# Turning group A's attention probabilities on VectorE, with value products in 32-row tiles

## The chip, the cores and the metric

The kernel runs on one core of one Trainium2 chip. Times are device microseconds (us) of one execution. A core has TensorE (PE: matmuls; its weight loads are shown apart as PEld), VectorE (DVE), ScalarE (ACT), GpSimd (POOL) and SyncE (SP, which here only issues DMAs), an on-chip memory SBUF of 128 partitions, and the accumulator memory PSUM with eight banks of 512 float32 columns. TensorE multiplies a stationary operand, loaded ahead as weights, with a moving operand, and sums over the partitions of the two.

## The reference

Two layers of an encoder on 1024 tokens of width 1024. Each layer normalizes, projects into four groups of attention heads (A to D), joins their outputs, projects back and adds, and then applies a squared-ReLU MLP of width 4096. Group A, which the change concerns, has four heads with keys of 96 and values of 64 columns and looks at all 1024 keys:

```python
def one_block(qi):                       # 128 queries at a time
    s = jnp.einsum('bqhd,bkhd->bhqk', qi, k, preferred_element_type=jnp.float32) * scale
    p = jax.nn.softmax(s, axis=-1)
    return jnp.einsum('bhqk,bkhd->bqhd', p.astype(v.dtype), v)
...
mix = jnp.concatenate([rms_norm(y_a, out_g_mla[l]), y_b,
                       rms_norm(y_c, out_g_swa[l]), rms_norm(y_d, out_g_na[l])], axis=-1)
x = x + mix @ w_out[l]
h = rms_norm(x, norm2_g[l])
x = x + jnp.square(jax.nn.relu(h @ w_up[l])) @ w_down[l]
```

All is float32. Group B has two softmaxes per head over all keys, C a band of keys, D a neighbourhood on a grid.

## The kernel before

Everything is planned before anything is emitted. The code calls engine operations on a `Plan`, which only records each as a step with its operands and what it depends on. `Plan.price` gives each step a cost, `Plan.order` then walks forward in time and picks for each engine, out of the steps whose inputs are ready, the one of lowest rank, if the places for its outputs are free; the steps are emitted in that order. A rank comes from the table `SPAN`: the steps of a stage (`"a"` for group A, `"o1"` and `"o2"` for the output projection, and so on) are spread over the stage's two numbers, so that a stage with earlier numbers goes first where both could run. The numbers are priorities and no times. `together()` makes several steps one unit that is emitted without a break.

Places are the SBUF and PSUM spaces that the plan gives out: 40 `pair` places of 1024 float32 columns a partition, 19 `half` of 512, small ones, and the 8 PSUM banks. `Place.tile` chooses the kind by size; a place goes back when the last step that uses its tile is done.

Group A, per head: four loads fill `stack` tiles (high and low parts of queries and keys, 96 rows), one load fills `v` ([128 keys, 8 blocks, 64]). For each of eight tiles of 128 queries, `softmax` runs six score matmuls of 512 columns into two `sb` banks, two VectorE reduces that move a bank to the SBUF tile `p` and keep the minimum (in the profile CUSTOM_DVE_ANT_0, each followed by a short read-out of the accumulator), and one ACT exponential over 1024 columns, which also gives the sum. `dense` then takes two query tiles at a time: eight 128x128 transposes of each on TensorE (`bank<-ident,p`) into `tr` banks, copies of 512 columns to `pt` tiles, in turn by VectorE and ACT (`transposed`), and eight value products with 64 stationary columns and 256 moving ones (`bank<-pt,v`), half of which write PSUM partitions 0 to 63 and half 64 to 127. `pv_out` adds the two halves: ACT copies one to `pvt`, VectorE adds it to the other into `y`. A float32 matmul is two records in the profile (each a weight load and a matmul); float32r, which scores and projections use, is one.

Of the output projection, products with `mix` (the split, normalized group outputs) belonging to groups B, D and C are in `o1`, since they don't need group A; the rest is in `o2`. In the MLP, operands split into a high and a low part lie in `pair` places (`near`, `far`).

Of the kernel before, what the change touches and what calls it, by code (L numbers as in the profile page):

```python
# [266 lines left out]
class Plan:  # L267
# [40 lines left out]
    def add(self, q, op, args, kw):  # L308
# [8 lines left out]
        s.start, s.tiled = None, False  # L317
# [51 lines left out]
    def price(self, s):  # L369
# [24 lines left out]
        if q == "tensor":  # L394
# [27 lines left out]
    def order(self):  # L422
# [30 lines left out]
        self.mode = False  # L453
# [119 lines left out]
    def issue(self, s, t):  # L573
# [13 lines left out]
        if q == "tensor":  # L587
# [13 lines left out]
            s.done = t + occ * (2 if s.tiled else 1) + 180 * (1.5 if slow else 1)  # L601
# [11 lines left out]
class Place:  # L613
# [9 lines left out]
    def tile(self, shape, dt, tag, bufs=None, name=None):  # L623
# [4 lines left out]
        kind = "pair" if n > 512 else "half" if n > P else "row" if n > 16 else "col"  # L628
# [8 lines left out]
class Trunk:  # L637
# [16 lines left out]
    PLACES = {"pair": 40, "half": 19, "row": 3, "col": 30, "bank": 8}  # L654

    def home(self, c):
        if c.kind in self.still:
            return self.still[c.kind][c.slot]
        n = 1024 if c.kind == "pair" else 512
# [239 lines left out]
    def attention(self, l):  # L899
# [51 lines left out]
        with at("open"):  # L951
# [84 lines left out]
        with at("o2"):  # L1036
# [13 lines left out]
    BANKS = {"mm": 8, "tr": 4, "sb": 2, "pv": 2}  # L1050
    EARLY, NP = 4, 6
    WAVES = [(T_BQ[t], T_BK[t], T_BV[t]) for t in range(2)]
# [134 lines left out]
    def latent_up(self, l, lat, rows, qa, ka, va):  # L1187
        nc, d = self.nc, self.d
        rq, rkv = self.big_tile(F, "rq"), self.big_tile(F, "rkv")
# [3 lines left out]
        for i, r in ((0, P), (1, 64), (2, P)):  # L1193
            p = []
            for j in range(2):
                t = self.big_tile(R, "latp")
# [163 lines left out]

    def attn_b(self, l, t, qb, kb, vb, out):
# [53 lines left out]
    def attn_a(self, l, qa, kn, krd, va, ys):  # L1415
# [3 lines left out]
        def head(h):  # L1419
# [13 lines left out]
            v = self.vtile(va[h])  # L1433
# [12 lines left out]
        yield from self.dense([lambda h=h: head(h) for h in range(4)])  # L1446
# [192 lines left out]

    def rows_split(self, t, src, scale=None):  # L1640

        self.split(t[0], t[1], src, scale)
        return t
# [22 lines left out]
    def mlp_up(self, l, acts):  # L1666
# [7 lines left out]
        with self.banks(u=2, p=2, q=2, mm=2):  # L1674
            near = lambda tag: [self.twin("op" + tag, R) for _ in range(4)]
# [118 lines left out]
            places = [near(c) for c in "abc"]  # L1794
# [58 lines left out]
    def mlp_down(self, l, acts):  # L1853
# [4 lines left out]
        with self.banks(u=4, p=4):  # L1858
# [4 lines left out]
            for j in range(4):  # L1863
# [12 lines left out]
                def op(o):  # L1876
                    return [self.rows_split(self.far(), t) for t in raw_op(o)]
# [130 lines left out]
```

## Time and profile before

| | us |
|---|---|
| median of three runs | 2522.7 (2518.65 to 2522.78) |
| profiled execution | 2517.78 |
| its span in the profile | 2516.0 |
| TensorE busy in the span | 2467.4 |
| VectorE / ACT / GpSimd busy | 1909.8 / 1290.5 / 379.7 |
| mean granted TensorE clock | 0.996 |

All helpers record through one line, so every group in the profile has the line L677, and groups are told apart by tile names: `out<-in`. A group's row gives the operation, its shapes, the count, then busy time and the mean ns of one, then the idle time of the engine before it with what ended it. A timeline row gives start, duration, engine and a count of like instructions in a row; its duration goes from the first start to the last end. Durations of matmuls include time in which the next one already streams.

### The profile page before, as it was taken

What the parts mean: (1) busy time and instruction counts of PE and PEld (TensorE: products, weight loads), DVE (VectorE), ACT (ScalarE), POOL (GpSimd) and SP (SyncE); (2) the same over time, 40 slices, a digit from 0 to 9 for tenths busy, and PEclk for the clock granted to TensorE, in tenths of its full rate; (3) what the DMA queues carried; (4) which work ended last, traced back from release to release, by engine and by line L of the source; (5) the groups of instructions that cost most, each with busy time, mean ns of one, the idle gap of its engine ahead of it and who ended that gap; (6) DMA issues with size and microseconds to landing.
All of it is one profiled execution on the core that took longest, in us unless ns stands there. A gap on an engine that the chain in (4) does not pass through costs nothing.

```text
span 2516.0 us, 35396 instructions
## 1 busy us (share of the span) xinstructions
PE 2467.4 (98%) x12332; PEld 1967.1 (78%) x12332; DVE 1909.8 (76%) x3576; ACT 1290.5 (51%) x2397; POOL 379.7 (15%) x258
## 2 busy tenths in 40 slices
PE   8999999999999999999999999999999999999998
PEld 6777776778888887888877777677788888888887
DVE  7767867775877779888777677677678777898887
ACT  4545757653644445444425456666455444444454
POOL 3323224213000000000042231332140000000000
PEclk9999999999999999999999999999999999999999
DMA  5534478622244457444154344885123444665431
GB/s 180 180 112 133 122 218 234 197 80 72 78 165 159 151 202 271 147 142 139 72 182 130 119 117 135 232 255 170 46 70 117 155 155 158 231 231 158 130 105 67
DMA packets 190514, 378.56 MB, mean 150 GB/s; under 512 B 24112, under 2 KB 36352, under 8 KB 190336
## 3 DMA queue, kind: packets, MB, share of 16 engines
q1 hardware_dynamic: 175360, 350.09, 44.6%
q10 hardware_dynamic: 14976, 26.22, 2.7%
q8 instruction: 97, 1.59, 0.3%
q14 instruction: 81, 0.66, 0.1%
HBM read 260.15 MB, written 116.07 MB: 150 GB/s over the span
## 4 chain that ended last, share of the span: by engine, by line
PE 83%; DVE 8%; DMA 4%; ACT 2%; issue 2%; SPq 1%; POOL 0%; DVEq 0%; POOLq 0%; ACTq 0%
PE bank L677 83%; DVE p L677 2%; DVE part L677 1%; SPq L677 1%; ACT p L677 1%; DVE x L677 1%; DMA a<-in_w_down 1%; DVE sq L677 1%; DMA acts<-ev 1%; DVE col L677 0%; DMA latp<-lat 0%; DMA c<-in_w_down 0%; DVE xl L677 0%; DVE ev L677 0%; DVE both L677 0%
## 5 line engine op out<-in xcount | busy, mean ns | idle before, releaser
L677 PE MATMUL bank<-far,wh 128*128 128x512 f32 (+1 forms) x2848 | 870.3, 387 | 1.1 <-ACT wh L677 0.6
L677 PEld LDWEIGHTS bank<-far,wh 128*128 128x128 f32 x2848 | 532.4, 188 | 110.5 <-ACT wh L677 1.4
L677 PE MATMUL bank<-far,wl 128*128 128x512 f32 (+1 forms) x1424 | 550.3, 387 | 2.7 <-DVE wl L677 2.7
L677 ACT ACTIVATE p<-p,col 128x1024 f32<-128x1024 f32 (+2 forms) x320 | 294.6, 921 | 196.3 <-DVE col L677 194.2
L677 POOL TENSOR_TENSOR wl<-ws,wh 128x512 fp32r<-128x512 f32 (+1 forms) x138 | 191.1, 1390 | 1180.2 <-ACT wh L677 1089.8
L677 PEld LDWEIGHTS bank<-far,wl 128*128 128x128 f32 x1424 | 267.4, 188 | 57.9 <-DVE wl L677 3.4
L677 PE MATMUL bank<-stack 96*128 96x512 f32 (+2 forms) x896 | 285.0, 395 | 5.0 <-DVE col L677 2.3
L677 DVE TENSOR_TENSOR x<-bank,x 128x512 f32<-128x512 f32 (+1 forms) x276 | 187.2, 680 | 121.9 <-PE bank L677 121.0
L677 PE MATMUL bank<-ident,p 128*128 128x128 f32 x1376 | 253.6, 276 | 10.4 <-DVE part L677 4.8
L677 PE MATMUL bank<-xh,wh 128*128 128x512 f32 x608 | 250.9, 413 | 3.1 <-ACT wh L677 2.6
L677 PE MATMUL bank<-xh,wl 128*128 128x512 f32 x608 | 250.6, 413 | 1.1 <-POOL wl L677 1.1
L677 PE MATMUL bank<-xl,wh 128*128 128x512 f32 x608 | 250.6, 412 | 0.0
L677 PEld LDWEIGHTS bank<-ident,p 128*128 128x128 f32 x1376 | 171.3, 141 | 59.5 <-issue 10.7
L677 PEld LDWEIGHTS bank<-stack 96*128 96x128 f32 (+1 forms) x896 | 159.3, 189 | 43.8 <-DVE col L677 12.1
L677 ACT ACTIVATE pt<-bank 128x512 f32<-128x512 f32 (+2 forms) x256 | 137.5, 556 | 82.9 <-PE bank L677 75.2
L677 DVE TENSOR_TENSOR wl<-raw,wh 128x512 fp32r<-128x512 f32 x224 | 150.3, 690 | 34.5 <-ACT wh L677 34.0
L677 PE MATMUL bank<-pt,v 128*64 128x256 f32 (+2 forms) x1344 | 173.1, 396 | 2.2 <-ACT pt L677 2.0
L677 ACT ACTIVATE ev<-ev 128x512 f32<-128x512 f32 x128 | 80.6, 632 | 160.3 <-DVE ev L677 155.8
L677 DVE CUSTOM_DVE_ANT_0 p<-bank,zero,col 128x512 f32<-128x512 f32 x192 | 143.8, 749 | 22.2 <-PE bank L677 5.1
L677 PE MATMUL bank<-mix,wh 128*128 128x512 f32 x512 | 160.3, 393 | 0.0
L677 DVE CUSTOM_DVE_ANT_0 p<-bank,zero 128x512 f32<-128x512 f32 x192 | 131.7, 686 | 35.4 <-PE bank L677 34.1
L677 ACT ACTIVATE wh<-raw 128x512 fp32r<-128x512 f32 x224 | 135.4, 621 | 23.8 <-ACT ev L677 10.5
(158 smaller groups left out, 3904.5 us busy)
## 6 DMA issues: line engine op xcount, KB each, us to landing
act<-acts SPq DMA_DIRECT2D x224, 256.0 KB
raw<-in_w_up SPq DMA_DIRECT2D x128, 256.0 KB
acts<-ev SPq DMA_DIRECT2D x128, 256.0 KB
acts<-ev ACTq DMA_DIRECT2D x96, 256.0 KB
ws<-in_w_in SPq DMA_DIRECT2D x76, 256.0 KB
c<-in_w_down SPq DMA_DIRECT2D x64, 256.0 KB
rz<-drows SPq DMA_DIRECT2D x40, 256.0 KB
ws<-in_w_out SPq DMA_DIRECT2D x40, 256.0 KB
```

What stands on the lines that cost most here:

```text
L677: getattr(s.eng.engine, s.op)(*[real(a) for a in s.args], **{k: real(a) for k, a in s.kw.items()})
```

## The change

For group A, `dense` is replaced by the new `turned`. Half a head (four query tiles) is taken at a time. For each query tile one VectorE instruction transposes all 32x32 blocks of `p` (128x1024) within their 32 partitions, into a wide tile `turn`: block row a of the queries lies on partitions 32a to 32a+31, and there each partition is a key. The value products then have 32 stationary rows: for each block of 32 keys and each of the four groups of 32 partitions a product of 32 rows, 64 stationary and 128 moving columns; even and odd key blocks write PSUM partitions 0 to 63 and 64 to 127, and each partition group writes its own bank (four `pq` banks). So eight tiles of the array are addressed, and 128 products make half a head, as one unit. The values must lie on all four partition groups, so `vrows` loads them four times, in eight DMAs a head. Each of the four banks is added up by ACT and VectorE as before, in pieces of 128 columns.

Besides, there are two `quad` places of 4096 columns a partition and 32 instead of 40 `pair` places. `turn`, the last four split operands of a layer's opening, six tiles of the stage before A, two operand sets of the MLP's up projection and four of seven in each quarter of its down projection lie in them. `SPAN` moves `a` to (400, 510) and `o1` to (430, 545). The price of a small float32 matmul is divided by the number of tiles.

```diff
@@ Plan.price
-                s.tiled = cols >= 128 and (out.arr.shape[0] <= 64 or s.args[1].arr.shape[0] <= 64)
-                if s.tiled:
-                    return max(4 * cols / 2.4 + 13, 224) / 2, cols / 2.4 * 2
-                return max(4 * cols / 2.4 + 13, 224), cols / 2.4 * 4
+                tiles = 128 // max(32, out.arr.shape[0]) * (128 // max(32, s.args[1].arr.shape[0]))
+                s.tiled = tiles if cols >= 128 and tiles > 1 else 0
+                tiles = max(s.tiled, 1)
+                return max(4 * cols / 2.4 + 13, 224) / tiles, cols / 2.4 * 4 / tiles
@@ Trunk
-    PLACES = {"pair": 40, "half": 19, "row": 3, "col": 30, "bank": 8}
+    PLACES = {"quad": 2, "pair": 32, "half": 19, "row": 3, "col": 30, "bank": 8}
@@ attention, opening
+            quads = [self.place.tile([P, 4, S], R, tag="quad", bufs=2, name="xq") for _ in range(2)]
-                h, lo = self.big_tile(R, f"xh{k}"), self.big_tile(R, f"xl{k}")
+                if k // 4 == l:
+                    h, lo = self.big_tile(R, f"xh{k}"), self.big_tile(R, f"xl{k}")
+                else:
+                    h, lo = (quads[k % 4 // 2][:, k % 2 * 2 + i] for i in range(2))
@@ SPAN
-            "d": (230, 390), "up": (335, 390), "c": (300, 405), "a": (405, 510), "mb": (345, 350), "md": (405, 410),
-            "mc": (415, 420), "ma": (515, 520), "o1": (505, 550), "o2": (550, 600), "mlp": (600, 1220)}
+            "d": (230, 390), "up": (335, 390), "c": (300, 405), "a": (400, 510), "mb": (345, 350), "md": (405, 410),
+            "mc": (415, 420), "ma": (515, 520), "o1": (430, 545), "o2": (550, 600), "mlp": (600, 1220)}
+    WIDE = {6, 4, 3}
@@ new
+    def vrows(self, src):
+        src = src.rearrange("(q r) k d -> r q (k d)", q=4)
+        tiles = []
+        for i in range(2):
+            v = self.place.tile([P, 2, 8, 64], F, tag="vr", bufs=4, name="v")
+            for a in range(4):
+                self.load(v[a * 32:a * 32 + 32].rearrange("p q k d -> p q (k d)"), src[:, 2 * i:2 * i + 2])
+            tiles.append(v)
+        return tiles
+    def turned(self, heads):
+        nc = self.nc
+        rows = [slice(a * 32, a * 32 + 32) for a in range(4)]
+        def products(job):
+            t, half, v, y, h2, done = job
+            pv = [self.bank("pq") for _ in rows]
+            with self.plan.together():
+                for n in range(16):
+                    for c in range(2):
+                        k, q = divmod(2 * n + c, 4)
+                        for r, ps in zip(rows, pv):
+                            nc.tensor.matmul(ps[c * 64:c * 64 + 64, 0:P], v[q // 2][r, q % 2, k], t[r, 2 * n + c],
+                                             start=n == 0, stop=n == 15)
+            o = y[h2 * 64:h2 * 64 + 64].rearrange("p (t a j) -> p a t j", a=4, j=32)
+            other = self.place.tile([P, 512], F, tag="pt", bufs=self.NT, name="pvt")[0:64]
+            for a, ps in enumerate(pv):
+                e = other[:, a * P:a * P + P]
+                nc.scalar.activation(e, ps[64:128, 0:P], AF.Copy)
+                self.tt(o[:, a, half * 4:half * 4 + 4], ps[0:64, 0:P].rearrange("p (t j) -> p t j", j=32),
+                        e.rearrange("p (t j) -> p t j", j=32), ALU.add)
+            if half:
+                done()
+        job = None
+        for head in heads:
+            probs, *rest = head()
+            for half in range(2):
+                t = self.place.tile([P, 32, P], F, tag="quad", bufs=2, name="turn")
+                for i in range(4):
+                    p = probs(half * 4 + i)
+                    nc.vector.transpose(t[:, :, i * 32:i * 32 + 32], p.rearrange("p (b j) -> p b j", j=32))
+                    if i == 1 and job:
+                        products(job)
+                job = (t, half, *rest)
+                yield True
+        products(job)
+        yield True
@@ attn_a
-            v = self.vtile(va[h])
+            v = self.vrows(va[h])
-        yield from self.dense([lambda h=h: head(h) for h in range(4)])
+        yield from self.turned([lambda h=h: head(h) for h in range(4)])
@@ mlp_down
-                    return [self.rows_split(self.far(), t) for t in raw_op(o)]
+                    to = self.wide() if o in self.WIDE else [self.far() for _ in range(4)]
+                    return [self.rows_split(p, t) for p, t in zip(to, raw_op(o))]
```

What the planner makes of it on TensorE, in the middle of group A in layer 0. `stack` rows are scores, `ident,p` transposes, `pt,v` value products, `mix` output projection. Before:

```order
L677 MATMUL bank_106<-stack 128x512 x3
L677 MATMUL bank_105<-ident,p 128x128 x4
L677 MATMUL bank_102<-ident,p 128x128 x4
L677 MATMUL bank_107<-stack 128x512 x3
L677 MATMUL bank_100<-stack 128x512 x3
L677 MATMUL bank_101<-ident,p 128x128 x2
L677 MATMUL bank_104<-ident,p 128x128 x2
L677 MATMUL bank_106<-ident,col_80 8x128
L677 MATMUL bank_105<-stack 128x512
L677 MATMUL bank_101<-ident,p 128x128 x2
L677 MATMUL bank_104<-ident,p 128x128 x2
L677 MATMUL bank_103<-pt,v 64x256 x8
```

No projection stands there; scores, transposes and products alternate. After, just ahead of the sixth batch of turned products:

```order
L677 MATMUL bank_106<-stack 128x512 x3
L677 MATMUL bank_101<-mix,wh 128x512
L677 MATMUL bank_101<-mix,wl 128x512
L677 MATMUL bank_100<-mix,wh 128x512 x2
L677 MATMUL bank_100<-mix,wl 128x512
L677 MATMUL bank_105<-stack 128x512 x3
L677 MATMUL bank_100<-mix,wh 128x512 x2
L677 MATMUL bank_102<-turn,v 64x128
L677 MATMUL bank_103<-turn,v 64x128
L677 MATMUL bank_107<-turn,v 64x128
L677 MATMUL bank_104<-turn,v 64x128
```

The transposes are gone and products of the output projection stand between the scores; between the first and the last turned product of a layer there are 138 of them, where before 13 stood ahead of the last value product of A. Between the first two batches of turned products of a layer, after, still on TensorE, there are scores and small column sums alone:

```order
L677 MATMUL bank_101<-stack 128x512 x3
L677 MATMUL bank_105<-ones,sq 128x1
L677 MATMUL bank_100<-stack 128x512 x3
L677 MATMUL bank_105<-ones,sq 128x1 x3
L677 MATMUL bank_104<-stack 128x512 x3
L677 MATMUL bank_107<-stack 128x512 x3
L677 MATMUL bank_105<-ones,sq 128x1 x2
L677 MATMUL bank_102<-stack 128x512 x3
L677 MATMUL bank_103<-stack 128x512 x3
```

The projection's first products stand behind the second batch. On VectorE, in the middle of group A (the ISA rows are the two reduces of a query tile and their read-outs), before:

```order
L677 COPY pt<-bank_104 128x512
L677 ISA p,col_88<-bank_102,zero 128x512
L677 ISA col_88 128x1
L677 ISA p,col_88<-bank_100,zero,col_88 128x512
L677 ISA col_88 128x1
```

and after:

```order
L677 TENSOR_TENSOR y<-bank_104,pvt 64x4x32
L677 COPY row_97<-bank_101 8x128
L677 STREAM_TRANSPOSE turn<-p 128x32x32
L677 ISA p,col_94<-bank_105,zero 128x512
L677 ISA col_94 128x1
L677 ISA p,col_94<-bank_103,zero,col_94 128x512
L677 ISA col_94 128x1
```

The block transposes stand among the reduces, in place of the copies out of PSUM.

More of the change, by code (lines that the diff above doesn't have):

```diff
@@ L1188, in latent_up @@
         nc, d = self.nc, self.d
-        rq, rkv = self.big_tile(F, "rq"), self.big_tile(F, "rkv")
+        quads = [self.place.tile([P, 4, S], R, tag="quad", bufs=2, name="latp") for _ in range(2)]
+        rq, rkv = (quads[1][:, i].bitcast(F) for i in (2, 3))
+        tiles = iter([quads[0][:, i] for i in range(4)] + [quads[1][:, i] for i in range(2)])
         self.spread(rq, rows[0], 0, 2)
@@ L1638, in twin, with wide @@
         return t[:, 0], t[:, 1]
+    def wide(self):
+        t = self.place.tile([P, 4, 2, 512], R, tag="quad", bufs=2, name="wide")
+        return [(t[:, k, 0], t[:, k, 1]) for k in range(4)]
     def rows_split(self, t, src, scale=None):
@@ L1674, in mlp_up @@
         with self.banks(u=2, p=2, q=2, mm=2):
-            near = lambda tag: [self.twin("op" + tag, R) for _ in range(4)]
+            near = self.wide
             far = self.far
@@ L1793, in mlp_up @@
                     combos(s.c)
-            places = [near(c) for c in "abc"]
+            places = [near(), near(), [self.twin("opc", R) for _ in range(4)]]
             ops[2] = [self.rows_split(places[0][k], x(k + 4, 0), gk(k + 4)) for k in range(4)]
@@ L1883, in mlp_down @@
                     t = raw_op(1)
-                b = [self.rows_split(self.far(), v) for v in t]
+                b = [self.rows_split(p, v) for p, v in zip(self.wide(), t)]
                 for m in M:
```

14 lines of the change are left out of this document (7 added, 7 removed).

## The prediction

> **What bounds the kernel now.** I read the busy times first, then the chain of waits, then the stretch in which group A runs, then single instructions in it. Busy times, and the shares of the chain that ended last:
> ```profile
> PE 2467.4 (98%) x12332; PEld 1967.1 (78%) x12332; DVE 1909.8 (76%) x3576; ACT 1290.5 (51%) x2397; POOL 379.7 (15%) x258
> PE 83%; DVE 8%; DMA 4%; ACT 2%; issue 2%; SPq 1%; POOL 0%; DVEq 0%; POOLq 0%; ACTq 0%
> ```
> TensorE is busy for 2467 of 2516 us and carries 83% of the chain, so time is won by taking work off TensorE, as far as it is not left waiting instead. The chain gives VectorE second place, and that is the engine that gets the new work. Group A's stage in each layer, by stretches (us, then busy time of PE, PEld, DVE, ACT, POOL, the granted clock, DMA share, GB/s):
> ```profile
> 443.00:557.00 114.00, 113.55 (x765) 85.16 (x763) 84.54 (x199) 76.87 (x133) 21.13 (x11) 1.00 0.46 140
> 1685.00:1799.00 114.00, 113.07 (x759) 84.80 (x761) 84.16 (x198) 76.12 (x132) 21.07 (x11) 1.00 0.47 138
> ```
> Both layers look alike: 114 us, TensorE without a gap at full clock, VectorE at 74%. What fills the first of them (groups: busy us, mean ns of one):
> ```profile
> L677 PE MATMUL bank<-ident,p 128*128 128x128 f32 x256 | 37.3, 275 | 0.1
> L677 PE MATMUL bank<-pt,v 128*64 128x256 f32 x260 | 31.8, 386 | 0.0
> L677 DVE CUSTOM_DVE_ANT_0 p<-bank,zero,col 128x512 f32<-128x512 f32 x32 | 24.0, 749 | 4.1 <-PE bank L677 0.6 <-DVE col L677 0.2
> L677 DVE CUSTOM_DVE_ANT_0 p<-bank,zero 128x512 f32<-128x512 f32 x32 | 22.0, 686 | 6.4 <-PE bank L677 6.3
> L677 DVE COPY pt<-bank 128x512 f32<-128x512 f32 x32 | 21.9, 686 | 11.9 <-PE bank L677 11.9
> L677 DVE TENSOR_TENSOR y<-bank,pvt 64x512 f32<-64x512 f32 x7 | 4.8, 680 | 0.1
> L677 DVE TENSOR_TENSOR y<-y,rz 128x1024 f32<-128x1024 f32 x1 | 1.2, 1221 | 0.0
> ```
> All 256 transposes of one layer's group A are in it, and practically all of its value products (256 records and a few of group C).
>
> **Transposes leave TensorE.** Matmuls overlap, so a busy time is not a price; the timeline gives the distance from start to start:
> ```profile
> 473.15 1.04 PE L677 MATMUL bank<-ident,p 128*128 128x128 f32 x8
> 473.94 1.61 PE L677 MATMUL bank<-stack 96*128 96x512 f32 x6
> 476.57 1.49 PEld L677 LDWEIGHTS bank<-pt,v 128*64 128x64 f32 x16 [0.22 <-issue]
> 476.58 1.95 PE L677 MATMUL bank<-pt,v 128*64 128x256 f32 x16
> 902.96 0.62 PE L677 MATMUL bank<-far,wh 128*128 128x512 f32 x2
> ```
> Eight transposes take 1.04 us with the last one 0.275 long: (1.04-0.275)/7 = 0.109 us each. 256 of them are 27.9 us a layer.
>
> **The value products.** A product is two records. Sixteen records of 256 columns take (1.95-0.386)/15 = 0.104 us each although each lasts 0.386: the two column tiles overlap fully, and a tile streams its 256 columns in 2 x 0.104 us. A batch is 16 x 0.104 = 1.7 us, and two make half a head: 3.3 us. The new batch for half a head is 256 records of 128 columns on eight tiles. If all eight overlap, each tile streams 32 records of half the length, 32 x 0.104 = 3.3 us, the same. No row shows four row tiles at work. Lower end: 3.3 us, since the tiles cannot stream faster. Upper end: 256 records one behind the other at the 0.104 us of the row, 26.6 us. I take 3.6 us, 0.3 above the lower end for filling eight tiles, because the row nearest to it, two tiles side by side, shows no loss from tiling. That is 2.4 us a layer more than before (8 x 0.3), while fewer changes between whole array and tiles (8 batches instead of 16 a layer; the 0.22 us of issue in the row is such a change) give back 8 times 0.4 (0.22 on entering, about as much on leaving), 3.2 us: together about 1 us less a layer.
>
> **VectorE gets 32 block transposes of 128x1024 a layer.** Before has none. Nearest row: one SBUF operation over 128x1024, 1.22 us (y<-y,rz). Lower end 0.69 (the 512-column copy, if 1024 went at twice its rate), upper end 2 x 1.22. I take 1.22: 39.0 us a layer. It loses 32 copies (21.9 us) and 8 sums of 64x512 (8 x 0.68 = 5.4). It gains 32 sums of 64x128; the smallest like operation is this, with its minimum of 0.416 us at 256 columns:
> ```profile
> L677 DVE TENSOR_TENSOR x<-x,rb x24: 416/420/685, 2495.8 to 2512.5; 128x256 f32<-128x256 f32 x16, 128x512 f32<-128x512 f32 x8
> L677 DVE TENSOR_TENSOR x<-bank,x x276: 417/689/696, 555.2 to 2504.9; 128x512 f32<-128x512 f32 x134, 128x256 f32<-128x256 f32 x4
> ```
> From 0.689 at 512 and 0.416 at 256 columns, 128 columns come to 0.28 us: 9.0 us. ACT loses 32 copies and gains short ones; at 77 of 114 us it stays out of the way. If that cover went it would cost the 32 small copies, under 10 us a layer.
>
> **The output projection moves into the stage.** By the order, 13 products on mix stood ahead of the last value product of A, now 138 stand between the first and last: 125 x (0.62-0.39 = 0.23) = 28.8 us of TensorE, and ten x sums of 0.69 on VectorE, 7 us. This is moved, not new.
>
> **The sum for a stage.** TensorE: 113.6 - 27.9 - 1 + 28.8 = 113.5 us. VectorE: 84.5 - 21.9 - 5.4 + 39.0 + 9.0 + 7 = 112.2 us. The two are level, so neither hides the other well. A turned half needs four score tiles reduced, exponentiated and turned first:
> ```profile
> 472.76 0.69 DVE L677 CUSTOM_DVE_ANT_0 p<-bank,zero 128x512 f32<-128x512 f32 x1 [0.73 <-PE bank L677]
> 473.61 0.75 DVE L677 CUSTOM_DVE_ANT_0 p<-bank,zero,col 128x512 f32<-128x512 f32 x1
> 474.40 1.15 ACT L677 ACTIVATE p<-p,col 128x1024 f32<-128x1024 f32 x1
> ```
> From the first reduce to the exponential's start are 1.64 us, so VectorE needs 4 x (1.64 + 1.22) + 4 x 0.28 = 12.6 us a half. Ahead of the second batch the order has only 24 scores (24 x (1.61-0.41)/5 = 5.8 us), the batch (3.6) and some small ones (2): 11.4, and the chain to the first turned tile adds about 3. So TensorE idles some 4 us at the start. In halves 4 and 5 (the order's instructions counted at these durations) the mix splits and x sums lie on VectorE too, 19 and 17 us against 12 and 16 on TensorE: about 4 more after the lead of the half before. I add 3 for single waits: 11 us. The stage takes 113.5 + 11 = 124.5 us and has done 28.8 us of later work: 114 - (124.5 - 28.8) = 18.3 us gained a layer, 36 in both.
>
> **Places and loads.** Two wide places hold what eight of the 40 pairs held, so the space is the same; a wide place comes free only when its last reader is done. Outside the stage the matmuls stand in the same rows but for a few. TensorE idles 2.6 us in the stretch over the layer border, where the new places first matter:
> ```profile
> 1240.00:1300.00 60.00, 57.41 (x267) 47.17 (x266) 50.68 (x55) 25.85 (x35) 19.56 (x10) 1.00 0.41 143
> 430.00:460.00 30.00, 29.69 (x188) 20.99 (x187) 21.77 (x53) 20.68 (x43) 8.75 (x6) 1.00 0.95 280
> 490.00:520.00 30.00, 30.00 (x212) 22.61 (x207) 24.81 (x58) 19.77 (x37) 4.73 (x2) 1.00 0.30 98
> L677 SPq DMA_DIRECT2D v<-va x8: 345/420/1073, 432.6 to 1720.3; - x8
> ```
> I price it at nothing, with ends of -2 and +5 us. Each head's values now come as eight transfers of 128 KB in place of one of 256 KB: 28 more issues of 0.42 us on SP and 3 MB more a layer, 11 us at 280 GB/s. Queues are 95% full at 430 to 460 us but at 30% from 490, and the first values are needed only after the first turned half; I price it at nothing, at 11 us a layer on the path if that cover fails. The instruction stream grows by 6100 instructions on TensorE. Before it came in 97 packets without a visible wait:
> ```profile
> q8 instruction: 97, 1.59, 0.3%
> ```
>
> **The prediction.** The profiled execution was 2517.8 us (span 2516.0), 4.9 under the median of the three runs, 2522.7; its terms are taken off the median: 2522.7 - 36 = 2487 us.
>
> **The rivals.**
> (1) Row tiles do not overlap freely: the four tiles of a column half take turns in loading weights. A 128-column load spaces the transposes at 0.109 us, so 64 columns cost 0.055; 128 loads in each half are 7.0 us a batch, 3.4 more than taken, 27 us a layer on TensorE. With little idle left (4 us): 113.5 + 27 + 4 - 28.8 = 115.7 against 114, or 2526 us. A limit on how densely records can start would do the same at 0.027 us each. For it: no row shows row tiles. Against: the two column tiles of the row load and stream side by side.
> [...]
> (2) The other side: all eight tiles take turns, or the engine cannot issue 512 instructions that fast. 256 x 0.055 = 14 us a batch, 83 us more a layer: 113.5 + 83 + 4 - 28.8 = 171.7 against 114, or 2638 us; the upper end of 26.6 us a batch would be later still. It decides from the point where a batch takes over 6.8 us, since 8 x 3.2 us then eat the gain with the idle time gone. For it: the densest stretch here is one record in 0.104 us, eight times sparser than needed.
> (3) VectorE's transpose runs at half rate, 2.44 us: VectorE then needs 112 + 39 = 151 us a stage and bounds it; with 4 us of lead, 155 - 28.8 - 114 = 12 us lost a layer, 2547 us. For it: no transpose on VectorE in this trace. Against: every 1024-column row here is near 1.2 us.
> [...]
> (4) The transposes go, but waits for wide places and values at layer border and stage start take half the gain: 2505 us. For it: DMA at 0.95; against: 0.3 us of idle TensorE there.
>
> **Chances.** Forecast 0.54, at 2470 to 2502; (1) 0.16, split over faster 0.04, same 0.05, slower 0.07; (2) 0.15; (3) 0.09; (4) 0.06. Faster: 0.54 + 0.04 + 0.06 = 0.64; same 0.05; slower 0.31. 0.2% (5 us) is about what can be told from no change here. The range leaves out (2) and a little at the low end: 2465 to 2560. Given a gain, it is 2465 to 2515.
>
> **What would show it.** The 512 transposes of A are gone from TensorE, and a batch of products takes 3.5 to 4 us; at 7 it is (1), at over 10 (2). A STREAM_TRANSPOSE row shows about 1.2 us; at 2.4 it is (3). TensorE's idle time in the stage, named VectorE, is about 11 us a layer; if it is 25 or more, the level sum was too kind to VectorE and the gain falls to some 9 us in all. Idle time at the layer border named DMA or a wide place speaks for (4).

## The result, and the profile after

The changed kernel takes 2557.8 us (median; 2550.9 to 2564.8) against 2521.7 us for the kernel before on the same chip: a ratio of 1.0145, 95% interval 1.0125 to 1.0165. The prediction was 2487 us, faster; the kernel is 36 us slower. The execution profiled has a span of 2561.8 us and a mean granted clock of 0.974 (before: 2516.0 us and 0.996).

Busy times of the changed kernel, and the shares of the chain that ended last:
```profile
PE 2459.8 (96%) x15404; PEld 1971.1 (77%) x15404; DVE 1950.0 (76%) x3624; ACT 1261.5 (49%) x2381; POOL 378.0 (15%) x258
PE 81%; DVE 10%; issue 3%; DMA 2%; ACT 2%; SPq 1%; POOL 0%; DVEq 0%; ACTq 0%; POOLq 0%
```
TensorE is 8 us less busy than before, although it lost 512 transposes, and the span is 46 us longer: the time lies in waits, and "issue" (TensorE idles, and the profile shows nothing that it waits for) has 3% of the chain in place of 2%. TensorE's waits (engine, what it wrote, what it waited for: us in total, times, longest):
```profile
PE bank L677 <- issue: 28.6, 15, 3.2
PE bank L677 <- ACT mix L677: 15.0, 4, 7.3
PE bank L677 <- DVE turn L677: 9.5, 4, 4.3
PE bank L677 <- DVE part L677: 9.4, 9, 2.7
```
The first three rows are new; the fourth was there before. Group A's stretch and what follows it (stretch, length, busy time of PE, PEld, DVE, ACT, POOL, then the granted clock, DMA share, GB/s):
```profile
470.00:490.00 20.00, 19.81 (x304) 16.22 (x303) 12.33 (x32) 7.37 (x16) 0.00 (x0) 0.63 0.16 45
510.00:530.00 20.00, 16.78 (x311) 13.67 (x311) 16.26 (x33) 9.25 (x18) 7.14 (x4) 1.00 0.56 152
590.00:610.00 20.00, 16.60 (x85) 13.27 (x85) 12.17 (x19) 4.83 (x13) 3.69 (x4) 0.91 0.16 49
610.00:630.00 20.00, 11.90 (x46) 9.55 (x47) 12.53 (x20) 8.63 (x17) 3.73 (x3) 0.74 0.17 53
```
TensorE looks busy at 470 to 490, but at a clock of 0.63. At 510 to 530 it idles 3 us with VectorE not full either, and of 610 to 630 it idles 8 us, again with no other engine full. Summed over the clock's own records, the changed kernel runs some 137 us at half clock, the kernel before 22 us. The parts that were priced from the nearest rows (groups: busy us, mean ns, idle before them):
```profile
L677 DVE STREAM_TRANSPOSE turn<-p 128x1024 f32<-128x1024 f32 x32 | 39.6, 1240 | 4.4 <-ACT p L677 4.3
L677 DVE TENSOR_TENSOR y<-bank,pvt 64x128 f32<-64x128 f32 x32 | 7.3, 277 | 19.5 <-ACT pvt L677 15.4 <-issue 4.0
L677 PE MATMUL bank<-turn,v 32*64 32x128 f32 x2048 | 37.6, 292 | 18.9 <-issue 14.2 <-DVE turn L677 4.7
```
VectorE's two prices are right to 2%. The third row carries 18.9 us of idle time, 14.2 of it named issue. Two batches of 256 records in TensorE's timeline, the fourth of layer 0 and the seventh of layer 1:
```profile
517.61 2.75 PE L677 MATMUL bank<-turn,v 32*64 32x128 f32 x175
523.58 1.44 PE L677 MATMUL bank<-turn,v 32*64 32x128 f32 x81 [3.22 <-issue]
```
```profile
1837.25 3.87 PE L677 MATMUL bank<-turn,v 32*64 32x128 f32 x256
```
The second is what the prediction priced (3.6 us from first to last start). The first stops after 175 records and waits for nothing that the profile shows. Of sixteen batches only this one reaches 3.6 us; layer 0's take 4.9 to 9.2 us, 49.5 in all. Fourteen of the sixteen stop for longer than 0.3 us, and each of these stops ends 1.2 to 1.6 us after a packet of 16 KB has landed in TensorE's instruction queue. The longest stops stand where the DMA engines are busy. Two stretches of 10 us, the first with a stop of 1.36 us from start to start, the second with the beginning of one of 3.51 (the number before the last is the DMA share):
```profile
570.00:580.00 10.00, 8.91 (x277) 7.64 (x278) 5.76 (x13) 5.03 (x11) 1.92 (x2) 1.00 0.02 5
580.00:590.00 10.00, 8.85 (x265) 7.34 (x263) 6.55 (x14) 3.75 (x6) 0.12 (x1) 1.00 0.82 261
```
No run changes the DMA load alone, so it is not shown that this load lengthens the stops.

A balance of one layer, worked out from the trace: each distance from a matmul's start to the next start is put down to the kind of the first, from the last product of the latent stage to the first product of layer 1 (us; the last two columns are experiments below).

| kind of matmul | before | after | cut | cut and mended |
|---|---|---|---|---|
| transposes and products on values | 61.5 | 4.3 | 4.3 | 4.3 |
| turned products | 0 | 51.3 | 41.9 | 40.6 |
| scores | 48.5 | 55.8 | 53.5 | 53.1 |
| products on mix | 88.4 | 94.4 | 94.9 | 91.8 |
| column sums and turned rows of the normalisations | 7.3 | 17.7 | 17.9 | 8.8 |
| all others (MLP) | 614.7 | 613.5 | 613.5 | 618.8 |
| sum | 820.4 | 837.0 | 825.9 | 817.3 |

The changed kernel loses 16.6 us in this layer. The 57.2 us taken away come back as 51.3; mix products, sums and rows cost 16.5 us more, scores 7.3. A wait counts in the row of the product ahead of it: the wait for mix in the rows, the wait for the first turned tile in the scores.

### The profile page after: what moved, and what is told of

Read it like the earlier page. It is cut to its first block, busy times and chain, and to the rows that moved or that the text cites. A ratio compares the mean times of both kernels' runs of the same rounds, so it can differ in the third digit from the quotient of the medians.

```text
span 2561.8 us, 41573 instructions
## 1 busy us (share of the span) xinstructions
PE 2459.8 (96%) x15404; PEld 1971.1 (77%) x15404; DVE 1950.0 (76%) x3624; ACT 1261.5 (49%) x2381; POOL 378.0 (15%) x258
## 4 chain that ended last, share of the span: by engine, by line
PE 81%; DVE 10%; issue 3%; DMA 2%; ACT 2%; SPq 1%; POOL 0%; DVEq 0%; ACTq 0%; POOLq 0%
PE bank L677 81%; DVE p L677 3%; DVE part L677 1%; DVE x L677 1%; DVE sq L677 1%; ACT p L677 1%; SPq L677 1%; DVE col L677 1%; DVE turn L677 0%; DVE acc L677 0%; DMA rz<-drows 0%; DMA latp<-lat 0%; DVE ev L677 0%; DVE both L677 0%; DMA stack<-kb 0%
## 5 line engine op out<-in xcount | busy, mean ns | idle before, releaser
L677 PE MATMUL bank<-far,wh 128*128 128x512 f32 x1792 | 552.8, 389 | 0.5 <-ACT ev L677 0.5
L677 PE MATMUL bank<-wide,wh 128*128 128x512 f32 (+1 forms) x1568 | 474.8, 385 | 0.0
L677 PEld LDWEIGHTS bank<-far,wh 128*128 128x128 f32 x1792 | 336.0, 188 | 70.8 <-ACT ev L677 1.3
L677 PE MATMUL bank<-far,wl 128*128 128x512 f32 x896 | 348.6, 389 | 0.0
L677 PEld LDWEIGHTS bank<-wide,wh 128*128 128x128 f32 x1568 | 292.4, 188 | 58.7
L677 PE MATMUL bank<-wide,wl 128*128 128x512 f32 (+1 forms) x784 | 301.6, 385 | 1.4 <-DVE wl L677 1.4
L677 PE MATMUL bank<-xq,wh 128*128 128x512 f32 x608 | 213.2, 415 | 0.0
L677 PEld LDWEIGHTS bank<-far,wl 128*128 128x128 f32 x896 | 168.2, 188 | 35.0
L677 PE MATMUL bank<-ident,p 128*128 128x128 f32 x864 | 179.4, 279 | 8.3 <-DVE part L677 4.1
L677 PEld LDWEIGHTS bank<-wide,wl 128*128 128x128 f32 x784 | 147.3, 188 | 31.5 <-DVE wl L677 2.2
L677 ACT ACTIVATE wh<-raw 128x512 fp32r<-128x512 f32 x224 | 135.9, 622 | 28.8 <-ACT ev L677 11.2
```

The lines of the kernel that those rows point to most:

```text
L677: getattr(s.eng.engine, s.op)(*[real(a) for a in s.args], **{k: real(a) for k, a in s.kw.items()})
```

## The experiments

Three theories stood at the start. F: TensorE runs out of instructions inside a batch. T (the tail): o1, moved into the stage, no longer covers group A's last normalisation. C: waits let the clock fall, and that is a loss of its own. A rival to F was that the small tiles hinder each other.

**Parts of the change by themselves.** The move alone, on the kernel before:
```
-"a": (405, 510) ... "o1": (505, 550)
+"a": (400, 510) ... "o1": (430, 545)
```


> The kernel before with one line changed: group A from 400 and o1 from 430 to 545, as in the changed kernel; the transposes stay on TensorE, no batch of small tiles. Theory T (the tail): o1 moved forward no longer covers group A's last normalisation, so TensorE waits for the mix chain after the last products, 9 us a layer as in the changed kernel, and the clock falls to half for some 10 us after it, about 5 us more of work lost: 2522 + 2 x 14 = 2550 us. Theory F (instruction fetch alone): nothing in this kernel is dense in instructions, so within 5 us of 2522.

2552.4 us, 1.0123 (1.0108 to 1.0138). TensorE's waits from 430 to 680 us, where the kernel before waits 0.4 us in all:
```profile
PE bank L677 <- ACT mix L677: 7.3, 1, 7.3
PE bank L677 <- DVE col L677: 1.2, 1, 1.2
PE bank L677 <- DVE mix L677: 1.0, 1, 1.0
```
The move by itself costs 32 us, about what T expected, with the same 7.3 us wait as in the changed kernel. Whether the wait is what costs is tested further on.

The turning without the move (the same two rows put back in the changed kernel):

> The changed kernel with the two rows of its table put back (group A from 405, o1 505 to 550). By the order some 80 products on mix again stand behind the last batch. Theory T: the 9 us wait at the tail of each layer goes, and with it the half clock behind it: 28 us less than the changed kernel where TensorE bounds the stage. But VectorE has 105 us of work in the stage against 85 on TensorE (both from the sums on record, without the moved products), so VectorE bounds the stage and TensorE idles 20 us a layer, some of it with half clock: about 2530 us. Theory F: the stalls of 1.4 to 3.5 us in each batch stay, but lie in time in which TensorE would have waited for VectorE anyway: 2530 to 2545 us. Both theories see the batch with its stall; only T sees the wait for the mix chain gone.

2589.0 us, 1.0271 (1.0255 to 1.0286): 44 us later than the latest time expected. The wait on mix falls to 1.4 us, as T said. The stage, before and here:
```profile
443.00:600.00 157.00, 156.54 (x962) 120.61 (x961) 105.16 (x228) 86.81 (x153) 31.65 (x21) 1.00 0.39 117
```
```profile
443.00:600.00 157.00, 128.29 (x2372) 105.04 (x2371) 107.41 (x232) 64.79 (x132) 25.69 (x16) 0.80 0.47 133
```
TensorE idles 29 us at a clock of 0.80, and VectorE is not full either (107 of 157 us). TensorE waits 12.4 us for issue and 15.7 for turned tiles, VectorE 7.9 for banks of scores: a batch that stalls holds up the scores, these hold up VectorE, and the next batch waits for it. So the moved products were worth 31 us to the turned kernel (2589.0 against 2557.8), although the same move costs 32 us in the kernel before.

Places alone: the changed kernel with group A's old functions and the old two rows.

> The changed kernel with group A as before (transposes on TensorE, products in pairs of tiles, one value tile a head) and the two rows of the table as before: what is left of the change are the two wide places in the projections, the latent stage and the MLP. My pricing at nothing: within 5 us of 2522. Rival 4 (waits for wide places at the layer border): 2530 us or more, with idle TensorE time named DMA or a wide place in the stretch over the layer border or the MLP.

2523.6 us, 1.0007 (0.9998 to 1.0017). The wide places cost nothing that can be told. This run loads the values once, as before, so it says nothing of their loads in four copies.

**Theory F.** Each batch is cut into four units, set between the next half's scores:
```
 with self.plan.together():
-    for n in range(16):
+    for n in range(4 * i, 4 * i + 4):
...
-if i == 1 and job:
-    products(job)
+for k in ((), (0,), (1,), (2, 3))[i] if job else ():
+    products(job, k)
```


> The changed kernel with each batch of 256 records cut into four units of 64 (128 instructions), emitted between the score tiles of the next half instead of in one row; nothing else. Theory F: TensorE ran out of instructions after about 350 in a row, so 128 in a row no longer stall: the 30 us of gaps inside batches fall under 5 us, the tail's wait stays; 2558 - 30 and some 10 us of half clock behind the stalls = 2515 to 2530 us. If the stall has another cause (the tiles themselves, the banks' write ports), 64 records keep a quarter of it each and the time stays at 2550 to 2560 us.

2531.5 us, 1.0042 (1.0028 to 1.0057): 26 us less than the changed kernel. Its stretches, and its waits from 430 to 660 us:
```profile
510.00:530.00 20.00, 20.00 (x380) 15.19 (x379) 17.71 (x34) 9.90 (x19) 6.38 (x3) 1.00 0.41 132
530.00:550.00 20.00, 20.00 (x379) 15.25 (x378) 15.58 (x35) 8.95 (x18) 1.98 (x2) 1.00 0.60 165
590.00:610.00 20.00, 11.47 (x50) 9.29 (x49) 9.39 (x15) 5.03 (x10) 1.46 (x2) 0.68 0.16 47
```
```profile
PE bank L677 <- ACT mix L677: 7.3, 1, 7.3
PE bank L677 <- DVE turn L677: 6.0, 2, 4.3
PE bank L677 <- issue: 3.1, 3, 1.8
```
The middle of the stage has no gap left; issue falls from 14.2 to 3.1 us, and the tail is as it was. Where units still stand side by side the stops stay: the longest of them (1.8 us) lies in three units in a row at 573 us. To see the instructions by themselves, a kernel with nothing but tiled products:

> Only the set-up and four stretches of small-tile products on TensorE, none of the reference's computation (the output is what was loaded of x, with four tiles of sums). Each stretch runs behind 60 products over the whole array and holds the same streamed columns, 160 rounds of 128 columns on eight tiles: 1280 records of 128 columns (2560 instructions), 640 of 256, 320 of 512, and the first again. All tiles full, a round of 128 columns takes 0.107 us as in the one undisturbed batch, so 17 us a stretch. Theory F (TensorE runs out of instructions): the 320 records take 17 us, the 640 somewhat more or 17, the 1280 at least 25 us, with gaps every 256 or so instructions behind packets of the instruction queue. Rival (the tiles disturb each other, whatever the instructions): all four stretches show gaps of the same length, or none.

(A product is two records, so each stretch has twice the records named there and 34 us at full rate.) Stretches of 128 columns took 71.4 and 73.0 us, the one of 256 columns 35.3 and that of 512 columns 34.0. TensorE's timeline at the start of the first, and the whole third:
```profile
20.57 6.02 PE L677 MATMUL bank<-x,rb 32*64 32x128 f32 x291 [4.76 <-DVE lam_e L677]
27.53 2.08 PE L677 MATMUL bank<-x,rb 32*64 32x128 f32 x128 [0.93 <-issue]
31.26 2.08 PE L677 MATMUL bank<-x,rb 32*64 32x128 f32 x128 [1.65 <-issue]
34.98 2.08 PE L677 MATMUL bank<-x,rb 32*64 32x128 f32 x128 [1.65 <-issue]
```
```profile
154.43 34.59 PE L677 MATMUL bank<-x,rb 32*64 32x512 f32 x640
```
The tiles do not hinder each other: the same columns run without a gap in records four times as long. With short records TensorE stops after 128 at a time (256 instructions with their weight loads; the first row holds 291), and each time a 16 KB packet of the instruction queue has landed 1.2 to 1.6 us ahead of the next 128, as in the changed kernel. A packet takes 0.9 to 1.4 us, yet they start 3.3 to 4.1 us apart, so no two overlap. The supply is 256 instructions in 3.5 to 4.0 us; the tiles use them up in 1.8 (128 records at 14 ns). Then bursts of such products between whole-array ones:

> Only the set-up and bursts of small-tile products of 128 columns, none of the reference's computation. Bursts of 64, 128, 256 and 512 records (a product is two records, which the expectation of the first such kernel counted as one), four of each, each behind 10, 20 or 40 products over the whole array (2.3, 4.5 and 9.1 us). Theory F, with the supply that the first such kernel showed (256 instructions in some 3.6 us while a tiled stretch uses them up in 1.7): 64 and 128 records run without a gap at 15 ns a record or less, 256 lose 1 to 4 us in some bursts as in the changed kernel, 512 lose 4 to 6 us in each, and a longer pause ahead helps the 256 but not the 512. Rival: the gap comes from the change between tiles and whole array, then each burst has it whatever its length.

All 24 bursts of 64 and 128 records run without a gap; of twelve of 256, eleven stop once, for 1.1 to 1.9 us from start to start (the rows give the idle part of it); those of 512 stop two or three times, whatever the pause. One of 128, and the first of 256:
```profile
54.22 2.09 PE L677 MATMUL bank<-x,rb 32*64 32x128 f32 x128
...
58.62 2.90 PE L677 MATMUL bank<-x,rb 32*64 32x128 f32 x185
62.90 1.35 PE L677 MATMUL bank<-x,rb 32*64 32x128 f32 x71 [1.37 <-issue]
```
From burst to burst the stop moves (behind records 185, 175, 165, 155): every burst of 256 with its ten products is ten records longer than two blocks of 128, so the stop stays at the same place of a block of 256 instructions. A pause of 40 whole-array products (9.1 us) helps no more than one of 10 (2.3 us); how far ahead TensorE fetches is not shown. F is shown, and the rivals are out. These kernels move next to no other data while they run (2 to 13 GB/s in all in the stretches of the first), and their stops stay under 2.3 us; the changed kernel's go up to 3.5.

**Theory T.** The changed kernel with output parts that need six of eight mix tiles put first (the first part of the edit):
```
 with at("o2"):
+    for m in front[:3]:
+        ws = self.weights(w_out[m, 0]) + self.weights(w_out[m, 1][:, 0:2])
+        held[m] = self.mm_ps()
+        share(held[m], m, 1, ws, range(6), stop=False)
     for m in back:
...
```


> The changed kernel with the second output stage in another order: the parts of three output blocks that need six of the eight mix tiles come first, into banks that are held, so 54 products stand ready while group A's last rows are normalised. Theory T: the wait for mix (7.3 + 1.2 us) and the half clock behind it go in both layers, 10 to 14 us a layer: 2530 to 2540 us. If the wait is not what costs (the time comes back later, or the banks held are missed elsewhere): 2550 to 2560 us.

2569.9 us, 1.0194 (1.0155 to 1.0234): no better, and later than either expectation. The wait stayed (7.6 us on mix): the order put all 54 of these products ahead of the normalisation's own last step (28 more than in the changed kernel ahead of its sums, 26 between sums and turned row), so the chain ended later. With cut batches:

> The batches cut into four units as in the spread kernel, and the output stage reordered as in the cover kernel. If stalls and tail are two independent losses, both gains add: 2531.5 - (20 to 28) = 2504 to 2512 us, faster than before by 0.3 to 0.7%. What is left then against the 2487 us on record is the wait of 4.3 us at each stage's start with the half clock behind it, some 20 us in all. If the stage is bound by VectorE anyway, the gain at the tail is partly given back: 2520 us.

2533.5 us, 1.0051 (1.0036 to 1.0066); the wait on mix is 5.9 us. With o1 from 410:

> As the one before, with o1 from 410 instead of 430, so that by the order some products on mix stand ahead of the first batch of small tiles, where TensorE waited 4.3 us for the first turned tile and then ran at half clock. Theory C (that wait and the clock behind it are the third loss): 5 to 10 us a layer less than the one before, 2485 to 2500 us. If the mix tiles come later than the order thinks, or group C's last products are held up by them, no gain: within 5 us of the one before.

2548.1 us, 1.0108 (1.0091 to 1.0125). The first wait shrank from 4.3 to 2.4 us, but the wait on mix is 7.8 us again and issue 5.5: units stood side by side once more. Then the normalisation's steps were let on earlier:
```
-s.slack = 5000
+s.slack = 1000 if self.stage == "ma" else 5000
```


> Batches in four units, output parts reordered, and group A's last normalisation steps let onto TensorE after 1 us instead of 5. Theory T: against the spread kernel (2531.5 us) the wait of 9 us a layer and 13.7 us of half clock behind it go, some 14 us a layer: 2500 to 2508 us, faster than before. If the wait for mix stays above 4 us: 2520 us or more.

2514.6 us, 0.9971 (0.9957 to 0.9986): faster than before by 0.3%, and 43 us faster than the changed kernel. Its waits from 430 to 680 us and the tail's stretch:
```profile
PE bank L677 <- DVE turn L677: 6.0, 2, 4.3
PE bank L677 <- issue: 2.4, 2, 1.5
PE bank L677 <- DVE wl L677: 1.7, 2, 1.2
```
```profile
590.00:610.00 20.00, 20.00 (x98) 16.67 (x97) 8.71 (x13) 6.67 (x15) 7.55 (x8) 1.00 0.27 82
```
The wait on mix is gone, and the half clock falls to 48 us. The same mending with whole batches:

> The changed kernel with its batches of 256 records whole, and only the tail mended as in the spread_chain kernel (output parts reordered, the last normalisation let on after 1 us). It fills the square of batches whole or cut and tail open or mended: 2557.8, 2531.5 and 2514.6 are the three others. If stalls and tail are independent: 2557.8 - 17 = 2541 us. If the stalls eat what the tail gives back: 2550 us or more.

2550.5 us, 1.0105 (1.0081 to 1.0129). By the medians, mending the tail gains 17 us with cut batches and 7 with whole ones. By the ratios it is 18 and 10 us, and the intervals leave some 9 us of doubt on the difference, so whether the two losses depend on each other is not settled. And on the move alone:

> The kernel with the move alone (o1 from 430, transposes on TensorE), and two mendings of the tail: the output parts that need six mix tiles come first, as in the cover kernel, and the steps of group A's last normalisation (its sums and its turned row) are let onto TensorE 1 us after the planner thinks their input ready, not 5 us. In the cover kernel 27 mix products that could have filled the wait stood ahead of those steps, so the chain itself began later and the wait stayed. Theory T: the chain of 25 us from the last value products to mix then runs under mix products, the wait of 7 to 10 us a layer and the half clock behind it go: 2552 - 28 = 2520 to 2528 us, no slower than before by more than 0.2%. If moving o1 costs for another reason: 2540 us or more.

2547.1 us, 1.0106 (1.0091 to 1.0122). Here T falls short: the wait on mix is 0.8 us at most, TensorE's waits from 430 to 640 us add up to 2.6 us, and still the move costs 26 us. In a balance of layer 0 like the one above, products on mix are 6.1 us dearer and all others (MLP) 7.7. Part of the latter is at the MLP's start, where nothing idled before:
```profile
640.00:700.00 60.00, 56.03 (x251) 45.12 (x250) 56.87 (x88) 39.62 (x73) 5.75 (x4) 0.97 0.20 66
```
So for the move alone the wait at the tail is seen, but its removal gave back 5 us by the medians, which the intervals of the two ratios (1.0123 and 1.0106) don't tell from nothing; why the rest stays is open.

**Theory C, and the price of a change of tiles.** On the cut and mended kernel: group C to 420, or group A from 385, to put other work under the first wait.

> As the one before, with group C's stage to 420 instead of 405, so that its last transposes and products stand among group A's first scores, where TensorE waits 4.3 us for the first turned tile. Theory C: that wait and the half clock behind it (6.8 us, and 3.4 us at 478) shrink by half or more: 4 to 8 us a layer less than the one before, 2488 to 2498 us. Rival: C's copies lie on VectorE, which is the late engine there, so the first turned tile comes as much later and nothing is won: within 5 us of the one before.

> As the spread_chain kernel, with group A's stage from 385 instead of 400: its first scores stand among group C's last work, and the first batch has more TensorE work ahead of it. Theory C: 4 to 8 us a layer less than spread_chain, 2488 to 2498 us. Rival: group A's loads (queues full at 430 to 460 us) come too late for it, and TensorE waits for a DMA or a value tile instead: within 5 us of spread_chain, or slower, with DMA named in the waits.

2528.0 us, 1.0027 (1.0016 to 1.0038), and 2527.6 us, 1.0022 (1.0006 to 1.0037). The wait on turn falls from 6.0 to 1.4 and 3.0 us, but issue rises from 2.4 to 7.1 and 4.9, and both kernels are 13 us slower than the one that they start from. For C to 420 neither expectation had that; for A from 385 the rival allowed it with DMA named in the waits, but a DMA is named for 0.2 us alone. Units of 128 records, idle products by the planner, and both:

> The spread_chain kernel with units of 128 records (256 instructions) instead of 64: 16 units a layer instead of 32. A change into tiles and back costs about 0.28 us there, so 16 fewer save 4.5 us a layer if nothing stalls. Theory F with a store of 256 to 350 instructions: units of 128 just fit, 2505 to 2510 us. If the store is smaller in practice, stalls come back in half of the units at 0.5 to 1 us: 2512 to 2525 us.

> The spread_chain kernel with 15 idle products over the whole array (3.4 us, a result that nobody reads) put between the scores of a layer's first half and its first unit, where TensorE waits 4.3 us for the first turned tile. Theory C (the wait itself is not to be had back, but the clock that falls behind it is): the 6.8 us of half clock at 457 and 1696 go, 2 to 3 us of work a layer: 2508 to 2512 us against 2514.6. If the clock falls for another reason, or the idle products come too late: 2515 to 2522 us.

> Units of 128 records and the idle products together. If both theories hold: 2500 to 2506 us, some 0.7% faster than before; if neither, 2515 us or more.

2530.6 us, 1.0044 (1.0030 to 1.0059); 2540.4 us, 1.0076 (1.0061 to 1.0091); 2529.4 us, 1.0032 (1.0020 to 1.0044). The first two are later than either of their expectations. All moved other work as well. With units of 128 the first two stand side by side, and stall as a whole batch did:
```profile
456.31 5.48 PE L677 MATMUL bank<-turn,v 32*64 32x128 f32 x196 [4.31 <-DVE turn L677]
463.40 1.16 PE L677 MATMUL bank<-turn,v 32*64 32x128 f32 x60 [1.61 <-issue]
```
So whether fewer changes of tile pay is not settled. Last, idle products with the order kept row for row:
```
+if s.op == "matmul" and s.args[2].cell.name == "turn":
+    if job is None or s.n - job > 4000:
...
+        for _ in range(15):
+            s.eng.engine.matmul(ps, z, z[:, 0:1].broadcast_to([P, 512]), start=True, stop=True)
```


> The spread_chain kernel with its order kept row for row, and 15 idle products over the whole array (3.4 us; the first real product overwrites them) put directly ahead of each layer's first tiled product, behind the order and not by the planner, so that nothing else moves. Theory C: TensorE's 4.3 us wait shrinks to about 1, the 6.8 us of half clock behind it goes in both layers, and the first two units run at full clock: 2 to 4 us a layer, 2506 to 2511 us against 2514.6. If the clock is not lost through that wait: 2512 to 2517 us.

2519.9 us, 0.9992 (0.9981 to 1.0003): no gain. The start of layer 0's stage:
```profile
454.79 2.13 PE L682 MATMUL bank<-zero 128*128 128x512 f32 x9
457.92 1.21 PE L684 MATMUL bank<-turn,v 32*64 32x128 f32 x64 [1.00 <-DVE turn L684]
...
464.34 1.44 PE L684 MATMUL bank<-turn,v 32*64 32x128 f32 x81 [1.39 <-issue]
```
The wait shrank to 1.0 us and the half clock at 457 us is gone, yet in the balance layer 0 takes 817.3 us with the idle products and without. Counted from the last product of the latent stage, the second to the eighth unit start 0.8 to 2.1 us earlier than without idle products, but from the twelfth on all start some 1.6 us later. Two stops of issue (1.39 and 0.55 us) and a wait of 0.9 us for VectorE's mix have come in between, where there were none or shorter ones. In layer 1 stops of 1.67 and 1.78 us stand behind the first units, 13.7 us of half clock follow them, and the units start 5.0 us later. So the idle products shift the stops, and C, as a loss of its own at the stage's start, is neither borne out nor refuted.

## Why the prediction was wrong

Two steps failed: the instruction stream priced at nothing, and the moved products priced as work alone.

- **Transposes leave TensorE: right.** The 256 a layer are gone.
- **The value products: the lower bound was right, the batch was mis-sized.** "If all eight overlap" holds: 3.6 us in the undisturbed batch. The term 8 x 3.6 = 28.8 us measured 51.3 us in the balance. What failed is a sentence further on: the instruction stream, 6100 instructions more, priced by "97 packets without a visible wait":
```profile
q8 instruction: 121, 1.98, 0.3%
```
  It is 121 packets now, still 0.3% of the time. The share says nothing of the wait: no two of the packets overlap (each takes 0.9 to 1.8 us, the closest start 3.4 us apart), and the undisturbed batch uses up 256 instructions in 1.8 us. Issue costs 28.6 us in waits, and cutting the batches gained 26 us.
- **Rival 1 had nearly the size, for another reason.** It gave 7.0 us a batch; layer 0's mean is 6.2 (49.5 / 8). But the loss is one stop a batch, 16.3 of the 20.7 us over 8 x 3.6, not slower records: the tiles start a record every 14 ns (3.6 us / 256). The rest lies in the first two batches, which ran in part at half clock (0.67 at 460 to 470 us, 0.50 at 470 to 480, 0.76 at 480 to 490). Rival 2 came nearer to the cause ("the engine cannot issue 512 instructions that fast"), with over twice the size, 14 us a batch.
- **VectorE: right.** 1.24 and 0.277 us against 1.22 and 0.28. Rival 3 is out.
- **The output projection "is moved, not new": this failed.** The 125 products were priced as work; that they had covered the chain from the last value products to mix was not. In its place stand a 7.3 us wait and some 9 us in all at each tail, and mix products, sums and rows are 16.5 us dearer in layer 0's balance. With cut batches the mending of the tail gave 17 us back, for the move alone nothing clear of noise, so how much of the move's cost is that wait stays open. The sum did need the move: without it the turned kernel is 31 us slower still.
- **11 us of idle time a layer: right at the start only.** 4 us at the start measured 4.3, which is most of the 7.3 us that scores are dearer. The other 7 did not come: waits named turn are 9.5 us in both layers together. That may be owed to the stops, which gave VectorE time.
- **Places at nothing: right** (1.0007, 0.9998 to 1.0017). No wait of TensorE names a load of values, so rival 4 is out as it was put. Whether the extra loads lengthen the stops, by the DMA load that they add, was not tested.
- **The sum.** Predicted for a layer: -18.3 us; measured for layer 0: +16.6. Of the 34.9 us between, transposes and products hold 23.0 (-28.9 became -5.9), mix, sums and rows 16.5. Scores, 7.3 dearer, and the MLP, 1.2 cheaper, stand in place of the 11 us of idle time that the sum had. The half clock has no line of its own: it lies in these rows, and 34.1 of layer 0's 37.5 us from 457 us on stand at or just behind a wait (6.8 us from 457, where TensorE waits 4.3 us for turn; 17.1 us from 468, behind the first batch's stop of 2.7 us; 10.2 us from 611, where it waits 7.3 us for mix). With both losses mended the kernel reached 2514.6 us, not 2487. In that balance the turned products still take 40.6 us, 11.8 over the term. Half of that, 5.9 us, is the way out of the tiles (29 times 0.197 us, where two records on tiles stand 0.007 us apart); the other half lies inside the units, stops and half clock among it. The way into the tiles (0.32 us in place of 0.23) counts in the rows of the products ahead.

## What to carry to other kernels

Splitting a product over small tiles keeps the columns and multiplies the instructions: count instructions per microsecond in the densest few microseconds, not in the whole program, and set other work between bursts of at most one block of 256 instructions. In whole kernels that made stops rare, not impossible: of units that stood alone, 3 of 54 of 64 records stopped (0.8 to 1.1 us idle, cut and mended kernel), and 4 of 24 of 128 records (0.4 to 1.3 us). When work is moved forward, ask which chain it covered where it stood, and whether the chain's own steps stand ahead of the cover in the queue. A resource with 0.3% of the time can still be the one that is waited for: no two packets of the instruction queue overlapped here, and 28.6 us of waits are named issue.

## What the runs showed of the hardware

TensorE took records on eight tiles of 32 by 64 at 14 ns a record (256 in 3.6 us, the undisturbed batch), but where a kernel held nothing but such products its instructions came at 256 in 3.5 to 4.0 us: 2560 records of 128 columns took 71 to 73 us where 640 of 512 columns took 34.0. With next to no other data moving, none of 12 bursts of 128 records stopped, bursts of 256 stopped in 11 of 12 cases, and a pause of up to 9 us ahead of a burst changed nothing. In that kernel and in the changed one the stops (those over 0.3 us) ended 1.2 to 1.6 us after a 16 KB packet of instructions had landed. In the bursts of 256 the stop's place moved with the instruction stream, by ten records from one burst to the next (185, 175, 165, 155). With the idle products that shortened the first wait from 4.3 to 1.0 us, a stop of 1.39 us stands in the third and fourth unit, where 0.1 us stood.
